# Three of eight feature tiles of a depthwise convolution as products with diagonal matrices

## The chip, the cores and the metric

One core of one Trainium2 chip. The time is that of one execution of the whole program on the device, in microseconds (us); of several runs the median is told.

## What is computed

A network of two blocks on 256 tokens of 1024 features, batch 1. The second block has two layers, and in layer 0 two streams go through the same mixer: the context (`ctx`) first, whose keys, values and states the latent stream's mixer then uses. In layer 1 only the latent stream has a mixer. Each mixer has three branches (attention, gated linear attention, convolution), which are gated, summed and projected:

```python
def _conv_module(glu, p):
    a, g = jnp.split(glu, 2, axis=-1)
    y = a * jax.nn.sigmoid(g)
    pad = CONV_WIDTH // 2                      # CONV_WIDTH = 31
    y = lax.conv_general_dilated(y, p['conv_w_dw'], (1,), [(pad, pad)],
                                 dimension_numbers=('NWC', 'WIO', 'NWC'),
                                 feature_group_count=CONV_CH) + p['conv_b_dw']
    y = jax.nn.silu(_layernorm(y, p['conv_ln_g'], p['conv_ln_b']))
    return y @ p['w_conv_o']
```

The convolution is depthwise: each of 1024 features has its own 31 taps over the tokens, and the layer norm after it runs over all features. So it needs all eight tiles of features.

## The kernel before, in words

Everything is kept with features on the 128 partitions and 256 tokens along them, so 1024 features are eight tiles (`KT`). A weight comes in units of 128x1024 f32 (`unit`, L438): SyncE loads `raw`, ScalarE rounds it to `whi`, VectorE or GpSimd subtracts to `wlo` (`load`, L455; in the mixer three of five subtractions go to GpSimd by `lo_eng`, L373). An ordinary product (`mm3`) is three runs of eight matmuls in the reduced format: `whi` with the high part of the input (`hh`, `yh`), `whi` with its low part (`hl`, `yl`), `wlo` with the high part; 24 matmuls to a unit. Their sums lie in three PSUM banks, `mm`. All small products (attention, gated linear attention or GLA) are in full f32, and their results share four PSUM banks of the pool `at` (`ps`, L414).

The convolution (`conv`, L1372) takes a tile `yp` of 128x286 (256 tokens with 15 zeros at each side), which `glu` (L1384) makes, and adds 31 taps on VectorE: one `tensor_scalar` with the first weight and the bias, then 30 `scalar_tensor_tensor` that multiply the shifted tile by a weight per feature and add it to the sum `ca`. The taps have a priority lowered by 1000, so that the scheduler puts them where VectorE has nothing else.

`mix` (L1395) sets the order in which the branches are written: a loop of 16 rounds with steps of attention (`att`), of `side` (the projections for GLA, with `glu` between), of the first GLA pair (`gla[0]`, one step for each of its eight levels) and of the convolution; then the first gated branch with the second GLA pair and the convolution; then the projections `r`, whose products with the GLA output make `yg`; then the second gated branch, the end of the convolution and its layer norm (`ln_core`, L603), and the third gated branch. This is not the order on the engines. A scheduler takes what is written, gives out the buffers of a pool in the order in which they are asked for, and lists the instructions of each engine by priority and its own estimate; each engine then runs its list in order.

Names in the rows: `mm` a projection's sum; `lg`, `pt`, `av` attention's logits, transposed weights and output; `gz`, `gt`, `gs`, `ga`, `ov` GLA's gates, transposition, state, scores of a level and output; `gF` a level's factors; `st` sums for norms; `hsq` squares; `fsum`, `sq` the layer norm's; `acc` the sum of the branches.

Of the kernel before, what the change touches and what calls it, by code (L numbers as in the profile page):

```python
# [10 lines left out]
F32 = mybir.dt.float32  # L11
# [3 lines left out]
AF = mybir.ActivationFunctionType  # L15
# [3 lines left out]
P = 128  # L19
D = 1024  # L20
T = 256
# [251 lines left out]
def run(*gens):  # L273
    for g in gens:
        for _ in g:
            pass


def step(g, n):
    for _ in range(n):  # L280
        if next(g, g) is g:
            return False
    return True
# [38 lines left out]
class Builder:  # L322
# [1046 lines left out]
                                       lambda ov, f=f + i: self.psplit(ov[:, :T], y[0][:, f], y[1][:, f]))  # L1369
                yield  # L1370

    def conv(self, l, yps, ca):  # L1372
        for ft, yp in enumerate(yps):
            o = ca[:, ft]
            w = lambda i: self.pvc(f"dw{l}", i * 8 + ft)
            self.ts(o, yp[:, 0:T], w(0), self.pvc(f"dwb{l}", ft), ALU.mult, ALU.add)
            for i in range(1, 31):
                with self.tc.high_priority(offset=-1000):
                    self.stt(o, yp[:, i:i + T], w(i), o, ALU.mult, ALU.add)
                if i % 8 == 7:  # L1380
                    yield
            yield

    def glu(self, l, h, yps):  # L1384
# [10 lines left out]
    def mix(self, l, h, x, ada, mem, bp, keep, then=None):  # L1395

        nc = self.nc  # L1400
        self.act(x, x, scale=ALPHA)
        qk, vg, glr, gates, pairs = self.gla_in(l, h, bp, True)
        S = mem[2] if mem else None
        new_S = None if mem else keep.tile([P, 2, 4, T], F32, tag="S", name="S")
        gla = [self.gla_pair(l, hp, qk, vg, glr, S, new_S) for hp in range(2)]
        run(gates)
        kt, vt = self.kv_in(l, h, bp if mem else keep, "x" if mem else "")
        if mem:
            self.rope(kt)
        yps = [bp.tile([P, T + 30], F32, tag="yp", name="yp", bufs=8) for _ in range(KT)]  # L1410
        newy = lambda: self.new_y(bp)
        ya = newy()
        ca = self.hp.tile([P, KT, T], F32, tag="D", name="ca")
        acc = None

        def gated(n, y):
            return self.gated_all(f"gb{n}_{l}", h, y, acc, n == 0, [0.0] * KT)
        att = self.attention(l, h, ya, kt, vt, mem, bp)
        conv = self.conv(l, yps, ca)
        side = chain(pairs[0], self.glu(l, h, yps), pairs[1])  # L1420
        step(att, 1)
        for i in range(16):
            step(att, 1)
            step(side, 1)
            step(att, 1)
            if i >= 2:
                step(gla[0], 1)
            if i >= 4:
                step(conv, 1)
        run(att, side, gla[0])  # L1430

        acc = bp.tile([P, 4, T], F32, tag="vg", name="acc", bufs=2)
        acc = [acc[:, f] for f in range(4)]
        for _ in range(2):
            a = bp.tile([P, 2, T], F32, tag="q", name="acc", bufs=2)
            acc += [a[:, 0], a[:, 1]]
        acc = Tiles(acc)
        g0 = gated(0, ya)
        for _ in range(8):
            step(gla[1], 2)  # L1440
            step(g0, 1)
            step(conv, 2)
        run(gla[1], g0)
        self.some_f32 = False
        yg = newy()
        for f in range(0, KT, 2):
            ps = self.pair(f"r{l}", f, h)
            s = self.t("sr", 512)
            self.act(s, ps, AF.Silu)
            for j in range(2):  # L1450
                sj = s[:, j * T:(j + 1) * T]
                if self.native:
                    self.tt(yg[0][:, f + j], sj, qk[:, f // 2, j], ALU.mult, nc.gpsimd)
                else:
                    self.tt(sj, sj, qk[:, f // 2, j], ALU.mult, nc.gpsimd)
                    self.split(sj, yg[0][:, f + j], yg[1][:, f + j])
            step(conv, 2)
        g1 = gated(1, yg)
        step(g1, 3)
        run(conv)  # L1460
        yc = newy()
        r = self.ln_core(ca, ca)
        for f in range(KT):
            t = self.t("ht")
            self.stt(t, ca[:, f], self.pvc(f"clg{l}", f), r, ALU.mult, ALU.mult)
            self.act(yc[0][:, f] if self.native else t, t, AF.Silu, bias=self.pvc(f"clb{l}", f))
            if not self.native:
                self.split(t, yc[0][:, f], yc[1][:, f])
            if f in (0,2,4,6):
                step(g1, 1)  # L1470
        g2 = gated(2, yc)
        run(g1)
        step(g2, 8)
        if then:
            step(then, 1)
        run(g2)
        mx = newy()
        self.halve(acc, mx)
        for f in range(0, KT, 2):
            if then:  # L1480
                step(then, 2)
            ps = self.pair(f"out{l}", f, mx)
            for j in range(2):
                self.stt(x[:, f + j], ps[:, j * T:(j + 1) * T], ada[:, 16 + f + j:17 + f + j], x[:, f + j],
                         ALU.mult, ALU.add)
        if then:
            run(then)
        run(self.post(x, f"l1g{l}", f"l1b{l}", l == 1))
        return kt, vt, new_S
# [148 lines left out]
```

## Time and profile before

| | us |
|---|---|
| median of 3 runs | 3063.51 |
| lowest and highest of them | 3053.55, 3064.5 |
| the profiled execution | 3057.49 |
| its span | 3055.3 |
| TensorE busy | 2805.1 |
| VectorE busy | 2004.4 |
| ScalarE busy | 1408.2 |
| GpSimd busy | 923.8 |

The span is what the profile shows of one execution, from its first instruction to its last; about 2 us lie around it. Busy times are of that execution alone, which is not one of the three runs. A busy engine isn't always the one that is waited for: what counts is which engine lets the others wait in the stage that is changed.

### The profile page before, as it was taken

The page shows a single profiled execution, that of the slowest core. Times are in us where ns is not written, and L with a number is a line of the kernel's source. Part 1 is how long each engine was busy: PE and PEld are TensorE (multiplying, and loading weights), DVE is VectorE, ACT ScalarE, POOL GpSimd, SP SyncE. Part 2 cuts the span into 40 slices and gives each one's busy share as a digit, 9 for nine tenths or more (in the row PEclk, how much of TensorE's full clock was granted, in tenths as well). Part 3 has the DMA queues.
Part 4 walks back from the last instruction along what each step waited for, and adds up shares of the span by engine and source line. Part 5 has one row for each costly group of instructions (what it writes and reads, how often), then busy time and mean ns, then how long its engine had stood idle before and what let it go on. Part 6 is the DMA issues. An engine that isn't in the chain of part 4 may idle for free.

```text
span 3055.3 us, 51829 instructions
## 1 busy us (share of the span) xinstructions
PE 2805.1 (92%) x20816; PEld 2626.8 (86%) x20816; DVE 2004.4 (66%) x3305; ACT 1408.2 (46%) x2127; POOL 923.8 (30%) x684
## 2 busy tenths in 40 slices
PE   7998889999998878799999999999999999998898
PEld 6897778888898778788899988998898788898898
DVE  7597763347855999956798344467344499674554
ACT  5464456544445434345645554445434332354443
POOL 3243322233324444641102104444320113453000
PEclk9999999999999989899999999999999999999999
DMA  5443334566456554688567986654643223344353
GB/s 196 146 159 130 125 112 177 179 250 246 154 203 237 193 211 173 238 304 287 210 233 249 330 307 254 239 188 172 250 147 119 97 97 124 118 161 144 126 180 109
DMA packets 153425, 578.32 MB, mean 189 GB/s; under 512 B 17628, under 2 KB 17756, under 8 KB 146656
## 3 DMA queue, kind: packets, MB, share of 16 engines
q1 hardware_dynamic: 152496, 574.45, 53.2%
q8 instruction: 163, 2.67, 0.3%
q14 instruction: 78, 0.64, 0.1%
q10 hardware_dynamic: 688, 0.56, 0.1%
HBM read 516.73 MB, written 58.20 MB: 188 GB/s over the span
## 4 chain that ended last, share of the span: by engine, by line
PE 46%; DVE 19%; ACT 4%; DMA 2%; issue 1%; POOL 1%; SPq 0%; DVEq 0%; ACTq 0%; POOLq 0%
PE mm L371 38%; DVE ca L364 7%; PE st L371 2%; DVE gF L361 2%; DMA raw<-in_ws 2%; PE av L371 1%; DVE sq L361 1%; PE ga L371 1%; DVE wlo L361 1%; PE ad L371 1%; POOL wlo L361 1%; DVE fsum L572 1%; ACT whi L358 1%; PE ov L371 1%; PE lg L371 1%
## 5 line engine op out<-in xcount | busy, mean ns | idle before, releaser
L358 ACT ACTIVATE whi<-raw 128x1024 fp32r<-128x1024 f32 (+1 forms) x706 | 735.9, 1045 | 838.5 <-PE mm L371 529.3
L361 POOL TENSOR_TENSOR wlo<-raw,whi 128x1024 fp32r<-128x1024 f32 (+1 forms) x282 | 717.1, 2545 | 1046.1 <-ACT whi L358 825.6
L361 DVE TENSOR_TENSOR wlo<-raw,whi 128x1024 fp32r<-128x1024 f32 (+1 forms) x315 | 397.7, 1263 | 356.9 <-ACT whi L358 345.8
L371 PE MATMUL mm<-hh,whi 128*128 128x256 f32 x3376 | 504.6, 291 | 18.9 <-ACT hh L358 5.5
L371 PE MATMUL mm<-hh,wlo 128*128 128x256 f32 x3376 | 495.7, 288 | 15.2 <-DVE wlo L361 10.1
L371 PE MATMUL mm<-hl,whi 128*128 128x256 f32 x3376 | 493.0, 288 | 0.0
L371 PEld LDWEIGHTS mm<-hh,whi 128*128 128x128 f32 x3376 | 448.9, 196 | 43.7 <-issue 9.0
L371 PEld LDWEIGHTS mm<-hh,wlo 128*128 128x128 f32 x3376 | 448.4, 196 | 18.5 <-DVE wlo L361 10.5
L371 PEld LDWEIGHTS mm<-hl,whi 128*128 128x128 f32 x3376 | 446.9, 195 | 3.8 <-issue 3.1
L364 DVE SCALAR_TENSOR_TENSOR ca<-yp,pv,ca 128x256 f32<-128x256 f32 x720 | 360.9, 556 | 2.0
L371 PE MATMUL mm<-yh,whi 128*128 128x256 f32 x1152 | 174.6, 291 | 14.6 <-ACT yh L358 10.1
L371 PE MATMUL mm<-h,raw 128*128 128x256 f32 x800 | 181.9, 381 | 0.0
L361 POOL TENSOR_TENSOR gF<-cum 128x128 f32<-128x128 f32 x192 | 99.8, 550 | 255.0 <-PE ga L371 142.0
L371 PEld LDWEIGHTS mm<-yh,whi 128*128 128x128 f32 x1152 | 154.6, 195 | 21.2 <-ACT yh L358 13.2
L371 PE MATMUL mm<-yh,wlo 128*128 128x256 f32 x1152 | 168.1, 288 | 4.9 <-DVE wlo L361 3.9
L371 PE MATMUL mm<-yl,whi 128*128 128x256 f32 x1152 | 168.7, 288 | 2.6 <-DVE yl L364 2.6
L371 PEld LDWEIGHTS mm<-h,raw 128*128 128x128 f32 x800 | 150.3, 191 | 19.3
L371 PEld LDWEIGHTS mm<-yh,wlo 128*128 128x128 f32 x1152 | 152.4, 196 | 6.8 <-DVE wlo L361 4.1
L371 PEld LDWEIGHTS mm<-yl,whi 128*128 128x128 f32 x1152 | 152.9, 195 | 3.3 <-DVE yl L364 2.8
L371 PE MATMUL mm<-hidh,whi 128*128 128x256 f32 x704 | 102.9, 287 | 0.5 <-ACT hidh L358 0.5
L371 PE MATMUL mm<-hidl,whi 128*128 128x256 f32 x704 | 102.2, 286 | 0.0
L371 PE MATMUL mm<-hidh,wlo 128*128 128x256 f32 x704 | 101.5, 285 | 0.0
(280 smaller groups left out, 3840.6 us busy)
## 6 DMA issues: line engine op xcount, KB each, us to landing
raw<-in_ws SPq DMA_DIRECT2D x744, 512.0 KB, 3.8
lo<-wlo SPq DMA_DIRECT2D x109, 512.0 KB, 3.0
wlo<-lo SPq DMA_DIRECT2D x109, 512.0 KB, 4.2
wada<-in_wa SPq DMA_DIRECT2D x48, 1024.0 KB, 5.9
raw<-in_ws SPq DMA_DIRECT2D x32, 384.0 KB, 3.0
memt<-in_tok SPq DMA_DIRECT2D x4, 256.0 KB, 4.7
xt<-in_tok SPq DMA_DIRECT2D x1, 1024.0 KB, 7.1
ct<-in_tok SPq DMA_DIRECT2D x1, 1024.0 KB
```

The source lines that it names most:

```text
L358: return self.nc.scalar.activation(out, in_, f, **k)
L361: return (eng or self.nc.vector).tensor_tensor(out=out, in0=a, in1=b, op=op)
L364: return self.nc.vector.scalar_tensor_tensor(out=out, in0=a, scalar=s, in1=b, op0=op0, op1=op1)
L371: return self.nc.tensor.matmul(out, lhsT=l, rhs=r, start=start, stop=stop, **k)
L572: self.nc.vector.tensor_reduce(out=s, in_=x.rearrange("p f n -> p n f"), axis=AX.X, op=ALU.add)
```

## The change

In layer 0's ctx mixer (the one whose `mem` is empty) `conv` leaves out tiles 2, 5 and 7, and `conv_pe` works them out. For each tap ScalarE writes a diagonal matrix (the identity, scaled by the tap's weight of each feature) into `dg`, which has two buffers of four matrices, and TensorE multiplies it by the shifted `yp` in full f32, 31 products summed in one half of a bank `cv` of the pool `at`. ScalarE adds the bias and writes the sum to `ca`. The products and the diagonals have the lowered priority of the taps. Two tiles share a bank, so there are two banks one after the other. The other two mixers are unchanged.

```diff
--- before.py
+++ after.py
@@ -1369,16 +1369,42 @@
                                        lambda ov, f=f + i: self.psplit(ov[:, :T], y[0][:, f], y[1][:, f]))
                 yield
 
-    def conv(self, l, yps, ca):
+    def conv(self, l, yps, ca, on_pe=()):
+
+        pe, n = self.conv_pe(l, yps, ca, on_pe), 0
         for ft, yp in enumerate(yps):
+            if ft in on_pe:
+                continue
             o = ca[:, ft]
             w = lambda i: self.pvc(f"dw{l}", i * 8 + ft)
             self.ts(o, yp[:, 0:T], w(0), self.pvc(f"dwb{l}", ft), ALU.mult, ALU.add)
             for i in range(1, 31):
                 with self.tc.high_priority(offset=-1000):
                     self.stt(o, yp[:, i:i + T], w(i), o, ALU.mult, ALU.add)
-                if i % 8 == 7:
+                if i % 8 == 7 or i == 30:
+
+                    n += 1
+                    if n > 3:
+                        step(pe, 1)
                     yield
+        run(pe)
+
+    def conv_pe(self, l, yps, ca, fts):
+
+        for k, ft in enumerate(fts):
+            if k % 2 == 0:
+                bank = self.ps("cv")
+            o = bank[:, k % 2 * T:k % 2 * T + T]
+            for i in range(0, 31, 4):
+                n = min(4, 31 - i)
+                dg = self.tmp[0].tile([P, 4, P], F32, tag="dg", name="dg", bufs=2)
+                with self.tc.high_priority(offset=-1000):
+                    for j in range(n):
+                        self.act(dg[:, j], self.cst("ident"), scale=self.pvc(f"dw{l}", (i + j) * 8 + ft))
+                        self.mm(o, dg[:, j], yps[ft][:, i + j:i + j + T], start=i + j == 0, stop=i + j == 30)
+                if i + n < 31:
+                    yield
+            self.act(ca[:, ft], o, AF.Identity, bias=self.pvc(f"dwb{l}", ft))
             yield
 
     def glu(self, l, h, yps):
@@ -1416,7 +1442,7 @@
         def gated(n, y):
             return self.gated_all(f"gb{n}_{l}", h, y, acc, n == 0, [0.0] * KT)
         att = self.attention(l, h, ya, kt, vt, mem, bp)
-        conv = self.conv(l, yps, ca)
+        conv = self.conv(l, yps, ca, () if mem else (2, 5, 7))
         side = chain(pairs[0], self.glu(l, h, yps), pairs[1])
         step(att, 1)
         for i in range(16):
```

How the order moves. Up to row 1250 TensorE's order is the same in both; from there TensorE's list before goes between the projections (`mm`) and the first GLA pair and attention (`lg`, `pt`, `av`, `ga`):

```order
L371 MATMUL lg<-kt,q 128x256 x2
L371 MATMUL ga<-gF 128x128 x4
L371 MATMUL mm<-hh,whi 128x256 x8
L371 MATMUL mm<-hl,whi 128x256 x8
L371 MATMUL mm<-hh,wlo 128x256
L656 MATMUL pt<-cc,pr 128x128
L371 MATMUL mm<-hh,wlo 128x256 x7
L371 MATMUL mm<-hh,whi 128x256 x8
L371 MATMUL mm<-hl,whi 128x256 x5
L656 MATMUL pt<-cc,pr 128x128 x3
L371 MATMUL mm<-hl,whi 128x256 x3
L371 MATMUL mm<-hh,wlo 128x256 x3
```

In the changed program projections alone follow there, 468 products in rows 1251 to 1320, and the end of that stretch reads so:

```order
L371 MATMUL mm<-yh,whi 128x256 x12
L371 MATMUL mm<-hh,whi 128x256 x8
L371 MATMUL mm<-hl,whi 128x256 x8
L371 MATMUL mm<-hh,wlo 128x256 x8
L371 MATMUL cv<-yp,dg 128x256
L656 MATMUL pt<-cc,pr 128x128 x4
L371 MATMUL mm<-yh,whi 128x256 x6
L371 MATMUL av<-ptsb,vt 128x256 x2
L371 MATMUL lg<-kt,q 128x256 x2
L371 MATMUL mm<-yh,whi 128x256 x3
L371 MATMUL cv<-yp,dg 128x256 x2
L371 MATMUL ga<-gF 128x128 x4
```

The attention head that stood at once behind row 1253 now stands behind the first convolution product, and with it the rest of the first GLA pair.

Further on TensorE's list before has the last levels of the second GLA pair, its output and norm between products of the first gated branch:

```order
L371 MATMUL mm<-hh,wlo 128x256 x8
L371 MATMUL mm<-yh,whi 128x256 x8
L371 MATMUL ga<-gF 128x128 x4
L371 MATMUL ga<-q_11995,qk 128x128 x4
L371 MATMUL mm<-yl,whi 128x256 x8
L371 MATMUL mm<-yh,wlo 128x256 x4
L371 MATMUL ov<-am,vg 128x256 x6
L371 MATMUL st<-hsq,ones 128x256 x2
L371 MATMUL ov<-am,vg 128x256 x2
L371 MATMUL mm<-yh,wlo 128x256 x4
```

and the changed one has them behind the projections `r` and 42 convolution products:

```order
L371 MATMUL mm<-hh,wlo 128x256 x8
L371 MATMUL cv<-yp,dg 128x256 x42
L371 MATMUL ga<-gF 128x128 x8
L371 MATMUL ga<-q_12094,qk 128x128 x4
L371 MATMUL cv<-yp,dg 128x256 x2
L371 MATMUL ov<-am,vg 128x256 x6
L371 MATMUL st<-hsq,ones 128x256 x2
L371 MATMUL ov<-am,vg 128x256 x2
L371 MATMUL cv<-yp,dg 128x256 x2
L371 MATMUL st<-hsq,ones 128x256 x2
L371 MATMUL cv<-yp,dg 128x256 x8
L371 MATMUL mm<-hh,whi 128x256 x8
```

They moved from within the first gated branch to behind most of `r`.

On VectorE, where before the taps stand in short runs between weight subtractions (`wlo`), levels (`am`, `gF`) and attention:

```order
L364 SCALAR_TENSOR_TENSOR ca<-yp,pv,ca 128x256 x5
L361 TENSOR_TENSOR wlo<-raw,whi 128x1024
L364 SCALAR_TENSOR_TENSOR ca<-yp,pv,ca 128x256 x5
L364 SCALAR_TENSOR_TENSOR yp<-gt,mm 128x256
L364 SCALAR_TENSOR_TENSOR ca<-yp,pv,ca 128x256
L1233 COPY_PREDICATED am<-gm,ga 128x2x2x128
L368 TENSOR_SCALAR ca<-yp,pv 128x256
L364 SCALAR_TENSOR_TENSOR ca<-yp,pv,ca 128x256 x5
L361 TENSOR_TENSOR wlo<-raw,whi 128x1024
L364 SCALAR_TENSOR_TENSOR ca<-yp,pv,ca 128x256 x6
```

the changed list has, while TensorE does the projections above:

```order
L361 TENSOR_TENSOR wlo<-raw,whi 128x1024
L364 SCALAR_TENSOR_TENSOR ca<-yp,pv,ca 128x256 x13
L361 TENSOR_TENSOR wlo<-raw,whi 128x1024
L364 SCALAR_TENSOR_TENSOR ca<-yp,pv,ca 128x256 x18
L361 TENSOR_TENSOR wlo<-raw,whi 128x1024
L364 SCALAR_TENSOR_TENSOR ca<-yp,pv,ca 128x256 x18
L361 TENSOR_TENSOR wlo<-raw,whi 128x1024
L361 TENSOR_TENSOR yl<-av,yh 128x256
L641 TENSOR_REDUCE nm<-lg 128x1
L364 SCALAR_TENSOR_TENSOR ca<-yp,pv,ca 128x256
```

The taps of the five tiles stand in long runs ahead of the attention's `yl` and `nm`, and the last of them right behind.

## Rows read from the trace of the kernel before

**Rows 1.** The page, part 1: busy time, share of the span, instructions.

```profile
PE 2805.1 (92%) x20816; PEld 2626.8 (86%) x20816; DVE 2004.4 (66%) x3305; ACT 1408.2 (46%) x2127; POOL 923.8 (30%) x684
```

**Rows 2.** The page, part 4: the chain of waits, share of the span by line.

```profile
PE mm L371 38%; DVE ca L364 7%; PE st L371 2%; DVE gF L361 2%; DMA raw<-in_ws 2%; PE av L371 1%; DVE sq L361 1%; PE ga L371 1%; DVE wlo L361 1%; PE ad L371 1%; POOL wlo L361 1%; DVE fsum L572 1%; ACT whi L358 1%; PE ov L371 1%; PE lg L371 1%
```

**Rows 3.** Windows: stretch, its us, busy us by engine, granted clock, DMA share, GB/s.

```profile
1036.90:1314.10 277.20, 219.45 (x1588) 211.81 (x1586) 261.37 (x411) 108.46 (x153) 142.29 (x112) 0.90 0.59 208
...
1036.90:1116.10 79.20, 67.23 (x480) 64.20 (x478) 78.70 (x148) 29.73 (x44) 31.41 (x28) 0.91 0.55 196
...
1198.00:1274.00 76.00, 60.02 (x456) 58.56 (x455) 72.25 (x99) 25.96 (x36) 48.20 (x32) 0.91 0.59 205
```

**Rows 4.** Tile `ca`, 989 to 1296 us: ns min/median/max, first start, last.

```profile
L364 DVE SCALAR_TENSOR_TENSOR ca<-yp,pv,ca x240: 459/474/2670, 989.1 to 1267.1; 128x256 f32<-128x256 f32 x120
...
L572 DVE TENSOR_REDUCE fsum<-ca x1: 3615/3615/3615, 1274.1 to 1274.1; 128x256 f32<-128x2048 f32 x1
...
L364 DVE SCALAR_TENSOR_TENSOR ca<-st,ca x1: 2278/2278/2278, 1279.9 to 1279.9; 128x2048 f32<-128x2048 f32 x1
```

**Rows 5.** Timeline of VectorE: start us, us, instruction, count.

```profile
1001.76 2.57 DVE L364 SCALAR_TENSOR_TENSOR ca<-yp,pv,ca 128x256 f32<-128x256 f32 x1
...
1049.51 1.26 DVE L364 SCALAR_TENSOR_TENSOR ca<-yp,pv,ca 128x256 f32<-128x256 f32 x3
...
1094.77 5.61 DVE L364 SCALAR_TENSOR_TENSOR ca<-yp,pv,ca 128x256 f32<-128x256 f32 x14
```

**Rows 6.** Timeline of GpSimd, around the first row above.

```profile
1001.44 2.60 POOL L361 TENSOR_TENSOR wlo<-raw,whi 128x1024 fp32r<-128x1024 f32 x1 [3.13 <-ACT whi L358]
```

**Rows 7.** Lines, 1036 to 1296 us: count, busy us, mean ns, idle before.

```profile
L364 DVE SCALAR_TENSOR_TENSOR ca<-yp,pv,ca 128x256 f32<-128x256 f32 x207 | 129.2, 679 | 0.2
...
L361 POOL TENSOR_TENSOR wlo<-raw,whi 128x1024 fp32r<-128x1024 f32 x33 | 98.5, 2988 | 63.0 <-ACT whi L358 33.8 <-ACT hsq L358 15.2 <-ACT gF L358 4.8
...
L361 DVE TENSOR_TENSOR wlo<-raw,whi 128x1024 fp32r<-128x1024 f32 x18 | 22.1, 1226 | 2.0 <-ACT whi L358 1.3 <-issue 0.6
...
L361 DVE TENSOR_TENSOR gF<-gF,qk 128x1024 f32<-128x1024 f32 x11 | 17.9, 1631 | 0.2 <-ACT gF L358 0.2
```

**Rows 8.** Timeline of TensorE: start us, us, instruction, count, idle before.

```profile
1037.96 1.12 PE L371 MATMUL mm<-hl,whi 128*128 128x256 f32 x8
...
1038.92 0.28 PE L371 MATMUL mm<-hh,wlo 128*128 128x256 f32 x1
...
1051.10 1.03 PE L371 MATMUL lg<-kt,q 128*128 128x256 f32 x4
...
1061.23 1.13 PE L371 MATMUL av<-ptsb,vt 128*128 128x256 f32 x4
...
1114.55 1.89 PE L371 MATMUL gz<-glr,w 128*128 128x256 f32 x8
...
1144.14 0.69 PE L1289 MATMUL gt<-cc,gw 128*128 128x128 f32 x2 [8.50 <-DVE gw L361]
...
1148.38 1.89 PE L371 MATMUL gs<-vg,gkt 128*128 128x256 f32 x8
...
1150.11 0.60 PE L1289 MATMUL gt<-cc,gw 128*128 128x128 f32 x4
...
1289.56 0.67 PE L371 MATMUL st<-sq,ones 128*128 128x256 f32 x2 [2.16 <-DVE sq L361]
...
1314.09 1.22 PE L371 MATMUL mm<-hh,whi 128*128 128x256 f32 x8 [2.17 <-DVE gt L364]
```

**Rows 9.** Lines by form, whole span: ScalarE's 128x128 activations.

```profile
L358 ACT ACTIVATE fs<-fs,fnm 128x128 f32<-128x128 f32 x16 | 6.3, 396 | 3.1 <-DVE fnm L939 3.1
...
L358 ACT ACTIVATE sw<-z 128x128 f32<-128x128 f32 x16 | 4.2, 261 | 0.0
```

**Rows 10.** Windows, tile `ca` alone, between two rows of TensorE above.

```profile
1114.55:1144.14 29.59, 13.30 (x22) 0.00 (x0) 0.83 0.58 206
```

## The prediction

> **What bounds the kernel now.** The page comes first: TensorE is busy for 92% of the span and VectorE for 66% [rows 1], so over the whole program TensorE is the bound. The chain of waits, read next, gives the place where that isn't so: the matmuls hold most of it, but second among its lines are the convolution's taps, `DVE ca`, with 7% [rows 2]. There are three mixers with a convolution, and only the first, the ctx mixer of layer 0, is changed. The busy time by stage is then read for it: from 1036.9 to 1314.1 us VectorE is busy 261.4 of 277.2 us and TensorE 219.5; in the first 79 us of that, VectorE has half a microsecond free [rows 3]. So here VectorE sets the pace and TensorE waits some 58 us (277.2 less 219.5). Of the convolution's own instructions the tile view shows 240 taps in this mixer, each 0.47 us in the median, and one of 2.67 [rows 4].
>
> I take that window because 1036.9 us is where TensorE's order first differs between the two programs, and 1314.1 us is the start of the first row from which on both have done the same products (row 1490 before, 1505 now).
>
> **What the change removes.** Three of eight feature tiles leave VectorE: 90 taps and 3 first taps. Fourteen taps in a row take 5.61 us [rows 5], 0.395 us each when they follow each other, so 93 x 0.395 = 37 us of VectorE. A tap that meets a GpSimd subtraction is longer: the one at 1001.76 takes 2.57 us and ends 0.3 us after the subtraction begun at 1001.44 [rows 5, 6]. The mean tap of this stretch is 0.679 us [rows 7], which over 207 taps is 42 us above the median tap, or 1.3 us for each of the 33 GpSimd subtractions; a single meeting costs 2.57 - 0.47 = 2.1.
>
> **What it adds.** 93 matmuls of 128x256 in full f32. Eight matmul records of that kind start 1.73 us before the next row, 0.216 each, and one product is two records [rows 8]: 0.43 us, so 40 us of TensorE. The ordinary product of this kernel (eight from 1037.96 to 1038.92 [rows 8]) is 0.12 us. So TensorE gets a little more than VectorE loses. ScalarE makes 93 diagonal matrices of 128x128; the two nearest rows are 0.261 and 0.396 us [rows 9]. I take 0.3, because an ordinary copy lies between: 28 us in all, 24 to 37 by the bounds, and below TensorE's 0.43 in each case. ScalarE has room, and on the way to the end it only counts where TensorE has nothing but these products. Three evictions on ScalarE (128x256) are some 1 us.
>
> **What it moves** decides. In the new order TensorE runs all that remains of the projections (`glu`, k, q and v of the second pair, the first gates), 468 products, before the first convolution product, and two attention heads, four levels of the first GLA pair and its output stand behind that; before, they stood in between. The convolution's bank comes from the same four PSUM banks (`at`), is asked for ahead of theirs, and its products have the lowest priority. In the same way the last two levels of the second GLA pair stand behind 42 convolution products in one row. VectorE on the other side does 107 of the 150 taps of its five tiles at a stretch. So the sum is made by stages, in TensorE's new order.
>
> 1. To the first convolution product's neighbours. TensorE needs 468 x 0.12 = 56 us. VectorE gets to its run of taps at about 1049.5, where before the attention's and level's work ends too [rows 5]. From there it has 107 taps (42.3), 8 weight subtractions at 1.14 without overlap (9.1; the row's 1.23 [rows 7] contains some) and 2 us of others: 53.3 us. GpSimd makes 11 subtractions meanwhile; at 1.7 us each, between the 1.3 and the 2.1 above, +19 (14 to 23). VectorE is done with it at 1122. TensorE waits for weights behind the runs of 20, 13 and 18 taps, arrives at about 1110 and then needs VectorE for the next attention maximum.
> The Trainium skill, "SBUF — State Buffer", section "Who interferes with whom", says that a VectorE instruction with two SBUF inputs and a GpSimd instruction that reads SBUF exclude each other, and that the later one waits for the whole of the other. By it alone each of the 11 would cost the full 2.1, and the sum would be 4 us higher; the rows agree on the exclusion, and the mean shows that not all of them meet a tap.
> 2. The postponed pieces, now one behind the other. From the logits to the product with the values took 10.1 us before (1051.10 to 1061.23 [rows 8]), some 3 of them taps; I take 8. Two levels of 4 us (the last multiplication alone is 1.63 in the mean, taps beside it [rows 7]; building and exponential come ahead of it), 1 us of copies, and 16 f32 products for output, norm and gates of the second pair (6.9): 24 us, to 1146.
> 3. The second GLA pair. From its gates' product to the first transposition took 29.6 us (1114.55 to 1144.14 [rows 8]), with 13 us of taps in between [rows 10]; without them 17. Of this stage's 58.8 us of products (384 ordinary ones 46.1, state and levels 9.7, seven of the convolution 3.0) 12.5 are done during the 17; the other 46, and 5 us of waits for six levels, follow: to 1214.
> 4. 54 convolution products 23.3, the last levels, output and norm 7.7, two waits of about 1 us: 33.5, to 1247.5. VectorE has next to nothing to do here.
> 5. 14 units of 2.88: 12 for the rest of r and the gates, 29 for y, then the last 19 convolution products 8.2: to 1296.
> 6. The layer norm over channels, which is now alone: in the new order no product stands between the last convolution product and the norm's two sums. Before it went from 1274.1 (the reduction) to 1289.6 (the second sum), 15.5 us [rows 4, 8], of which some 5 went to other work. I take 11, with 3.6 and 2.3 for the two long instructions [rows 4]: to 1307.
> 7. Five units 14.4: to 1321.5, against 1314.1 now: **7.5 us later**. The norm's result then comes 17 us before it is wanted where before it had 28: 3 us more of waiting (0 to 8).
>
> Sum: +40 us of products on TensorE, and 30 of its waits go: **+10.5 us** on 3057.5 us, the profiled execution's time. That execution is 6.0 us below the median of the three runs (3063.5), so on the median I write 3074. The forecast's own range is the bounds above: VectorE's meetings with GpSimd 4 us either way, stage 3's waits 0 to 12, stage 6 at 9 to 15, stage 2's levels at 3 to 5 us, and stage 1 up to 12 us shorter if GpSimd fits into gaps: 3053 to 3092. Nothing else is charged: the weight loads and their queue are the same transfers in the same order, and the first two groups of diagonals are made far ahead, on an idle ScalarE.
>
> **The rivals.** *The relief arrives* (faster). VectorE's 261 us fall by 37 and by a share of the meetings; TensorE needs 219.5 + 40 = 259.5, of which some 22 are time at the lower of its two clock levels (the granted clock is 0.90 of full here [rows 3]) behind waits. With full speed in most of the stretch and 20 us of waits instead of 58 it takes 237 + 20 = 257 instead of 277, and the time is 3043. For it speaks that VectorE really is the limit in every stage of rows 3. Against it speaks that the removed 37 us are needed evenly, while the new order gives VectorE its taps all in stage 1 and leaves it empty in stages 4 and 5.
>
> *The diagonal products set the pace* (slower). In stages 4 and 5, 73 of these products stand in rows with little else. There are two buffers of four diagonals; TensorE uses a group in 1.73 us. If a diagonal takes 0.396 us [rows 9] and the hand-over to and fro adds 1 us to each group, a group takes 2.6, and 15 groups cost 13 us more. The lower clock costs 22 us in this stretch now, in which TensorE's timeline has a dozen waits of over 2 us, so about 2 us each; six new ones are 12 more. With the forecast's +10.5 that is +35: 3099. It decides once ScalarE needs over 0.43 us a diagonal with its waits. For it: every such group crosses engines twice. Against it: ScalarE is less than half busy in all of these stages.
>
> *The edit doesn't take effect* is excluded by the order: 93 products fewer on VectorE and 93 on TensorE. That the mixer's end is hidden is excluded too: the next mixer starts with its result, and the chain of waits runs through it.
>
> **Chances.** The forecast 0.50, of which most lies within 15 us of the median, since it is +10.5 with bounds of -10 and +28; the relief 0.14; the diagonals 0.28; and 0.08 for other mixtures, near no change. A measurement of this kernel can tell about 0.5%, 15 us, from no change. That makes faster 0.13, same 0.47, slower 0.40. The range goes from the relief's time to the diagonals': 3040 to 3102.
>
> **What would show it.** Right: VectorE's taps in a dense block up to about 1122, TensorE waiting 15 us or so for weights in it; attention and levels behind 1110; 42 `cv` products in a row near 1215 with VectorE idle; a wait of about 10 us before the norm's sums, near 1300. Wrong: taps without meetings and a first convolution product before 1100 (then the relief), or `cv` products more than 0.5 us apart (then the diagonals).

## The result, and the profile after

Four runs of the changed kernel had a median of 3087.2 us (3084.55 to 3094.24) beside 3059.6 for the kernel before: a ratio of 1.0084, 95% interval 1.0067 to 1.0101. It is **0.84% slower**, some 26 us; the two profiled executions are 3084.55 and 3057.49 us. The forecast was +10.5 us. The page, part 1, beside [rows 1]:

```profile
PE 2839.2 (92%) x21002; PEld 2657.3 (86%) x21002; DVE 1949.2 (63%) x3212; ACT 1438.2 (47%) x2223; POOL 925.4 (30%) x684
```

VectorE lost 55 us, TensorE gained 34, and the span grew by 27. The windows of the changed mixer (stretch, its us, then busy us of PE, PEld, DVE, ACT, POOL, granted clock, DMA share, GB/s) answer to [rows 3]; the last row is the whole of it, from the row where the orders part to the first row after which both have done the same products:

```profile
1036.90:1116.10 79.20, 62.13 (x462) 61.05 (x461) 76.94 (x134) 24.03 (x31) 43.20 (x22) 0.87 0.62 219
1116.10:1153.20 37.10, 32.00 (x192) 28.05 (x191) 23.64 (x49) 16.72 (x35) 10.19 (x16) 0.95 0.49 179
1153.20:1225.70 72.50, 62.51 (x471) 60.84 (x470) 54.29 (x75) 37.73 (x49) 43.69 (x43) 0.93 0.61 220
1225.70:1258.50 32.80, 32.24 (x160) 27.59 (x159) 6.70 (x9) 20.40 (x57) 1.42 (x7) 1.00 0.19 65
1258.50:1312.20 53.70, 50.58 (x374) 48.73 (x373) 21.96 (x21) 25.32 (x46) 31.41 (x20) 0.97 0.74 268
1312.20:1348.10 35.90, 19.71 (x125) 17.96 (x124) 20.68 (x33) 13.47 (x26) 10.60 (x8) 0.71 0.27 90
1036.90:1348.10 311.20, 259.16 (x1773) 244.22 (x1771) 204.20 (x318) 137.66 (x241) 140.51 (x112) 0.91 0.54 192
```

The stretch takes 311.2 us instead of 277.2. TensorE is busy for 259.2 instead of 219.45, which is the forecast's 40 us; but it still waits 52.0 us where it waited 57.7. VectorE was to be freed and is: 204 of 311. TensorE hardly profits.

TensorE's timeline shows the places (start us, us, instruction, count, idle before):

```profile
1073.92 2.07 PE L371 MATMUL mm<-hh,wlo 128*128 128x256 f32 x8 [6.09 <-DVE wlo L361]
...
1117.63 0.60 PE L371 MATMUL cv<-yp,dg 128*128 128x256 f32 x2
...
1151.48 1.03 PE L371 MATMUL gz<-glr,w 128*128 128x256 f32 x4
...
1172.03 0.66 PE L1289 MATMUL gt<-cc,gw 128*128 128x128 f32 x2 [6.10 <-DVE gw L361]
...
1225.72 4.92 PE L371 MATMUL cv<-yp,dg 128*128 128x256 f32 x22
1231.20 13.65 PE L371 MATMUL cv<-yp,dg 128*128 128x256 f32 x62 [0.56 <-ACT ca L358]
...
1303.96 8.37 PE L371 MATMUL cv<-yp,dg 128*128 128x256 f32 x38
...
1316.52 1.22 PE L371 MATMUL st<-fsum,ones 128*128 128x256 f32 x2 [4.19 <-DVE fsum L572]
...
1324.35 1.19 PE L371 MATMUL st<-sq,ones 128*128 128x256 f32 x2 [6.61 <-DVE sq L361]
...
1329.99 2.08 PE L371 MATMUL mm<-hh,whi 128*128 128x256 f32 x8 [4.45 <-DVE gt L364]
...
1348.12 1.22 PE L371 MATMUL mm<-hh,whi 128*128 128x256 f32 x8 [0.96 <-DVE gt L364]
```

and VectorE's timeline the other side of it:

```profile
1079.21 12.30 DVE L364 SCALAR_TENSOR_TENSOR ca<-yp,pv,ca 128x256 f32<-128x256 f32 x20
...
1110.40 3.45 DVE L361 TENSOR_TENSOR wlo<-raw,whi 128x1024 fp32r<-128x1024 f32 x1 [2.26 <-ACT whi L358]
...
1125.68 0.42 DVE L361 TENSOR_TENSOR yl<-av,yh 128x256 fp32r<-128x256 f32 x1
...
1245.78 0.73 DVE L1233 COPY_PREDICATED am<-gm,ga 128x512 f32<-128x512 uint8 x1 [18.51 <-PE ga L371]
...
1312.87 3.59 DVE L572 TENSOR_REDUCE fsum<-ca 128x256 f32<-128x2048 f32 x1 [7.31 <-ACT ca L358]
```

All that the forecast named is there: the block of taps to 1125.7; waits for weights (`wlo`) in it; the convolution's row of 42 products (two records each, 22 and 62) with VectorE idle for 18.5 us; the norm's sums with nothing to cover them. After them, behind waits of 4.19, 6.61 and 4.45 us, the granted clock is 0.71 of full in the mean of the last stretch, between the two levels, and eight products take 2.08 us at 1329.99 against 1.22 at 1348.12.

The row at 1348.12 answers to the one of before at 1314.09 [rows 8]: 34.0 us later. Of these 5.5 come back in the next 90 us, where TensorE waits 6.1 us in all instead of 8.5 and has a granted clock of 1.00 in the first 52 us against 0.97; 27 are left at the end.

### The profile page after: what moved, and what is told of

Same layout as the page of the kernel before. It is cut to its first block, busy times and chain, and to the rows that moved or that the text cites. A ratio compares the mean times of both kernels' runs of the same rounds, so it can differ in the third digit from the quotient of the medians.

```text
span 3082.6 us, 52227 instructions
## 1 busy us (share of the span) xinstructions
PE 2839.2 (92%) x21002; PEld 2657.3 (86%) x21002; DVE 1949.2 (63%) x3212; ACT 1438.2 (47%) x2223; POOL 925.4 (30%) x684
## 5 line engine op out<-in xcount | busy, mean ns | idle before, releaser
L364 DVE SCALAR_TENSOR_TENSOR ca<-yp,pv,ca 128x256 f32<-128x256 f32 x630 | 300.7, 539 | 2.2
```

The lines of the kernel that those rows point to most:

```text
L364: return self.nc.vector.scalar_tensor_tensor(out=out, in0=a, scalar=s, in1=b, op0=op0, op1=op1)
```

## The experiments

Each kernel is compared with the kernel before on the same chip. Told is the ratio of the times with its 95% interval in brackets, and the ratio as microseconds of 3062, about the median of the kernel before.

**The first four kernels.** The first theory was *order*: the 40 us of products are paid for by VectorE's relief, and what costs is where the scheduler put things. Its rivals were *products* (40 us on TensorE cost what they cost anywhere) and *diagonals* (the hand-over from ScalarE).

`normal_priority`, in `conv_pe`:

```diff
-                with self.tc.high_priority(offset=-1000):
+                if True:
```

> The change with one edit: the convolution's products and diagonals are written at normal priority instead of the lowered one; VectorE's taps keep theirs. In TensorE's list attention and the levels then stand where they stood before the change, with four convolution products between one level and the next, and all 93 are done ahead of the second GLA pair's output. Theory 'order' (what costs is that attention, levels and norm were put behind projections and products, not the 40 us of products themselves): faster than before by 15 us (0 to 25). Rival 'products' (40 us more on TensorE cost what they cost wherever they stand): still 20 to 30 us slower than before. Rival 'diagonals' (the hand-over from ScalarE sets the pace): still 15 to 27 us slower, since the same 93 diagonals are made.

Measured: 1.0026 (1.0015 to 1.0038), +8.0 us. No theory had that: undoing the order is worth some 18 us, but leaves a kernel that is still slower.

`quarter_products`:

```diff
-                    for j in range(n):
+                    for j in range(1):
...
-                        self.mm(o, dg[:, j], yps[ft][:, i + j:i + j + T], start=i + j == 0, stop=i + j == 30)
+                        self.mm(o, dg[:, j], yps[ft][:, i + j:i + j + T], start=i == 0, stop=i == 28)
```

> The change with one product and one diagonal of every four: 24 instead of 93. Left out are the other 69 taps of tiles 2, 5 and 7. TensorE's order is the one of the change (bank asked for ahead, lowered priority, 468 projections first, two levels behind the second gated branch's r), only that the norm's sums stand 123 projections further back, as in the kernel before. 'order': 69 products less, at 0.43, are 30 us less on TensorE, but only those that stand in rows (some 54 of them, 23 us) and the exposed norm (12 us) come off the time: 5 to 10 us faster than before, and 20 us or more slower than the kernel without any of the products. 'products': the change's +27 less 30, 3 us faster than before, and 10 us slower than the kernel without products.

Measured: 0.9966 (0.9952 to 0.998), 10.4 us faster.

`constant_matrix`:

```diff
-                dg = self.tmp[0].tile([P, 4, P], F32, tag="dg", name="dg", bufs=2)
+                pass
...
-                        self.act(dg[:, j], self.cst("ident"), scale=self.pvc(f"dw{l}", (i + j) * 8 + ft))
-                        self.mm(o, dg[:, j], yps[ft][:, i + j:i + j + T], start=i + j == 0, stop=i + j == 30)
+                        self.mm(o, self.cst("ident"), yps[ft][:, i + j:i + j + T], start=i + j == 0, stop=i + j == 30)
```

> The change with the constant identity in place of the diagonals: no diagonal is made on ScalarE, the 93 products stay and the order of TensorE too. Left out are the tap weights of tiles 2, 5 and 7. 'order' and 'products': within 5 us of the change, 22 to 30 us slower than before. 'diagonals': 10 to 20 us faster than the change.

Measured: 1.0089 (1.0073 to 1.0106), the same as the change. *Diagonals* is out. The tile view says it too, of the change's diagonals and of this kernel's products (ns min/median/max):

```profile
L358 ACT ACTIVATE dg<-cc,pv x93: 384/387/402, 863.8 to 1309.9; 128x128 f32<-128x128 f32 x93
```

```profile
L371 PE MATMUL cv<-yp,cc x186: 377/378/631, 1120.3 to 1313.9; 128*128 128x256 f32 x186
```

`no_products`, in `conv_pe`:

```diff
-            for i in range(0, 31, 4):
...
-            self.act(ca[:, ft], o, AF.Identity, bias=self.pvc(f"dwb{l}", ft))
+            for i in range(0, 28, 4):
+                yield
+            self.act(ca[:, ft], yps[ft][:, 15:15 + T], AF.Identity, bias=self.pvc(f"dwb{l}", ft))
```

> The change without bank, diagonals and products: ScalarE fills the three tiles from the middle of yp. Left out is the convolution of tiles 2, 5 and 7. TensorE's order is that of before to within a few projections. It bounds the relief on VectorE. 'order': VectorE's 37 us and a share of the meetings come off a stretch that VectorE bounds, 35 us faster than before (25 to 45). 'products': the change's +27 less 40 us of products, 13 us faster than before (8 to 18).

Measured: 0.9935 (0.9921 to 0.995), **19.9 us faster**, neither 35 nor 13. With 37 us of taps gone, the meetings that went with them, and nothing in their place, 20 us is all that is won. And `quarter_products`, in the change's order with 10 us of products, is only 9.5 us behind it: *order* as first stated falls too, since an order that costs 20 should show there.

Why only 20? The view of TensorE's waits (waiting line, released by: us in total, times, longest), for the changed stretch of the kernel before:

```profile
PE mm L371 <- DVE wlo L361: 14.0, 3, 9.3
PE ga L371 <- DVE gF L361: 9.3, 3, 4.8
PE gt L1289 <- DVE gw L361: 8.5, 1, 8.5
PE mm L371 <- POOL wlo L361: 5.9, 3, 4.8
PE ov L371 <- DVE am L1239: 5.6, 1, 5.6
PE pt L656 <- DVE nm L361: 4.3, 1, 4.3
```

and of `no_products`:

```profile
PE ga L371 <- DVE gF L361: 7.9, 4, 3.0
PE mm L371 <- DVE wlo L361: 6.4, 1, 6.4
PE ov L371 <- DVE am L1239: 6.2, 1, 6.2
PE gt L1289 <- DVE gw L361: 6.2, 2, 4.7
PE st L371 <- DVE sq L361: 5.3, 1, 5.3
PE pt L656 <- DVE nm L361: 4.4, 1, 4.4
```

Waits for **weights** (`wlo`), which stand behind the taps on VectorE, were 19.9 us and are 6.4. The waits for levels, gates, attention's maximum and output (27.7 us in these rows) are as long as before to within 3 us in all. I read them as chains across engines, each step waiting for the last, beside which VectorE's taps only filled the time; that is argued. So the second theory, *few waits*: only the waits for weights can be won, and everything that TensorE gets is paid from those 20 us.

**The next four.** `own_bank` separates the two parts of the order:

```diff
-        self.atp = ep(name="atp", bufs=4, space=bass.MemoryType.PSUM)
+        self.atp = ep(name="atp", bufs=3, space=bass.MemoryType.PSUM)
+        self.cvp = ep(name="cvp", bufs=1, space=bass.MemoryType.PSUM)
...
-                bank = self.ps("cv")
+                bank = self.cvp.tile([P, 512], F32, tag="cvb", name="cv")
```

> The change with a PSUM bank of its own for the convolution's products, taken from the pool of attention and levels, which keeps three; products and diagonals keep the lowered priority. Attention and all levels then stand in TensorE's list where they stood before the change, but 42 products stand in one row right ahead of the norm's two sums, with no product between these. So this has the exposed norm of the change without its postponed attention and levels. 'order' splits its 20 us (the change less the kernel at normal priority) into the norm, some 12, and the postponed work, some 8: 20 us slower than before (14 to 25). Rival 'all of it is the bank' (attention and levels asked for behind the convolution's bank are the whole 20): 8 us slower than before, like the kernel at normal priority. Rival 'lowered priority in itself': no less than the change's 27.

`before_three_banks` is its control, with only the 4 of the first line made 3, in the kernel before:

> The kernel before with three instead of four PSUM banks for attention and levels, nothing else: what the bank that the kernel above takes away costs. All theories: within 4 us of before. If it is more, the kernel above is read against this one.

Measured: 1.0073 (1.0058 to 1.0088), +22.4 us, and 1.0 (0.999 to 1.001) for the control. With attention and the levels back in place nearly all of the loss stays, so the bank and its queue are the smaller part. (The interval overlaps the change's own, 1.0067 to 1.0101.) The norm remains as the candidate.

`one_tile`: `normal_priority` with `(2,)` for `(2, 5, 7)`.

> One tile (2) instead of three on TensorE, at normal priority: 31 products, four after each level of the first pair. The kernel without products was 20 us faster, which is the 20 us that TensorE waited for weights behind the taps; its other 34 us of waits stayed. Theory 'few waits' (only the waits for weights behind the taps can be won, and the first tile taken off wins most of them): 12 us of relief less 13.3 us of products, of which a third comes back with the clock: 3 us faster than before (0 to 7). Rival 'relief in proportion' (each tile gives 6.5 us and costs 9): 3 us slower.

Measured: 0.9978 (0.9966 to 0.9989), **6.7 us faster**, at the upper end of what *few waits* had. The waits for weights in this stretch are now

```profile
PE mm L371 <- DVE wlo L361: 7.2, 3, 3.0
```

7.2 us instead of 19.9: of the waits for weights the first tile wins most.

`one_tile_placed`: the same, but the groups of products are taken out of `conv` and written where TensorE waited:

```diff
+        self.fill = self.conv_pe(l, yps, ca, on_pe)
...
+        if not hp:
+            step(self.fill, 3)
         st = self.st()
...
+            if hp and li in (0, 1, 2, 4, 5):
+                step(self.fill, 1)
             ps = self.ps("ga").rearrange("p (h b n) -> p h b n", h=2, n=P)
```

> One tile (2) at normal priority, its 31 products written where TensorE waited before for something other than weights: 12 right ahead of the first pair's output (5.6 us of wait), 8 at the second pair's transpositions (8.5 us), 11 between its levels (9.3 us). 'few waits': the relief of the kernel above, and the first 12 products, 5 us, lie in a wait: 8 us faster than before (3 to 12). 'relief in proportion': 1 us faster. If the place of the products is of no account: the same as the kernel above.

Measured: 0.999 (0.9981 to 1.0), 3 us faster: a miss, since 8 were expected. The wait that the products were to fill grew from 8.5 to

```profile
PE gt L1295 <- DVE gw L361: 12.1, 1, 12.1
```

since the scheduler now lists 78 projections between the gates and the transposition where it had 113. From gates to transposition takes 26.8 us here and 29.6 before [rows 8].

**The last four.** `norm_covered`, in `conv_pe`:

```diff
-                with self.tc.high_priority(offset=-1000):
+                with self.tc.high_priority(offset=-500):
```

> The change with one number: the products' and diagonals' priority is lowered by 500 instead of 1000. Attention and the first pair's levels still stand behind projections (524 of them instead of 660), the last two levels of the second pair still behind r, but the last products end some 90 projections ahead of the norm's two sums, which stand where they stood before. Theory 'norm' (most of what order costs is that no product stands between the convolution's end and the norm's sums): 11 us better than the change, 14 us slower than before (8 to 18). Rival 'postponed' (attention and levels behind projections are most of it): 22 to 27 us slower than before.

Measured: 1.0045 (1.003 to 1.0059), **+13.8 us**, as *norm* had it. Attention and levels are still postponed, and 12 of the 26 us are gone. TensorE's timeline shows the last product well ahead of the sums, and short waits at them, and the view of its waits has another change:

```profile
1274.94 7.07 PE L371 MATMUL cv<-yp,dg 128*128 128x256 f32 x32
...
1293.00 0.59 PE L371 MATMUL st<-fsum,ones 128*128 128x256 f32 x2
...
1303.18 1.05 PE L371 MATMUL st<-sq,ones 128*128 128x256 f32 x2 [2.16 <-DVE sq L361]
...
1329.10 1.22 PE L371 MATMUL mm<-hh,whi 128*128 128x256 f32 x8 [2.00 <-DVE gt L364]
```

```profile
PE mm L371 <- DVE wlo L361: 8.4, 2, 6.1
```

The waits at the norm (for `fsum`, `sq` and the `gt` behind them) are 4.2 us here and 16.2 in the change, which is the 12 us. But the waits for weights are also shorter, 8.4 us where the change has 17.1, and those for levels and `yl` longer (12.5 against 7.9): the edit moved all the products, so the norm's share is not shown alone.

`two_tiles`: `normal_priority` with `(2, 5)`.

> Two tiles (2 and 5) at normal priority, 62 products. 'few waits' (only the some 20 us of waits for weights can be won, and the first tile takes most of them): the second tile costs 9 us (13.3 less a third) and wins 3 to 4: 1 us faster to 3 slower than before. 'relief in proportion' (each tile moves the time by as much as the first, which gave 7): 14 us faster.

Measured: 0.9988 (0.9979 to 0.9997), 3.7 us faster, somewhat better than *few waits* had it. The first tile gave 6.7, the second takes some 3 back (the two intervals overlap), the third 11.7 more. *Relief in proportion* is out.

`one_tile_both_mixers`: `normal_priority` with `(2,) if l == 0 else ()`. The lines of the kernel before from 1487 to 1674 us, which hold the latent mixer's convolution (busy us, mean ns | idle before), have all 240 taps and not one weight subtraction:

```profile
L364 DVE SCALAR_TENSOR_TENSOR ca<-yp,pv,ca 128x256 f32<-128x256 f32 x240 | 103.3, 483 | 0.8
```

> One tile (2) at normal priority in both mixers of layer 0, the ctx and the latent one. In the latent mixer of the kernel before VectorE does the same 240 taps, at 0.483 us in the mean, and TensorE has no wait for weights at all from 1360 to 1800 us. 'few waits': nothing can be won there, so the 31 products cost their 13 us or a little less: 5 us slower than before (2 to 8), which is 12 slower than with one tile in the ctx mixer alone. 'relief in proportion' to the taps taken off VectorE: 13 us faster than before.

Measured: 1.0013 (1.0004 to 1.0023), +4.0 us, 10.7 behind `one_tile`. The same edit on the same taps wins 6.7 us in the ctx mixer and loses 10.7 in the latent one, where TensorE waits for no subtraction. (It does wait 8.2 us for rounded weights, `whi`, from ScalarE between 1360 and 1800 us, so the expectation's "no wait for weights at all" is too strong.) What this run can't tell is which waits made the difference: in the latent mixer TensorE hardly waits for anything, being busy for 181.2 of the 187 us from 1487 to 1674, where in the ctx mixer it is 219.5 of 277.2.

`one_tile_lowered`: the change with `(2,)` for `(2, 5, 7)`.

> The change with one tile (2) instead of three, at its lowered priority: attention and the first levels stand behind 660 projections as in the change; the last product ends 92 projections ahead of the norm's sums. 'norm': the order costs little where the norm is covered: 2 us faster than before (5 faster to 3 slower), 5 us behind the same tile at normal priority. 'postponed': 12 us behind it or more, so at least 5 us slower than before.

Measured: 0.9978 (0.9967 to 0.9989), 6.7 us faster, level with `one_tile`, where 2 us and 5 behind it were expected. And *few waits* as stated doesn't explain it: in this kernel TensorE waits 25.0 us for weights, more than the 19.9 of before,

```profile
PE mm L371 <- DVE wlo L361: 18.8, 4, 8.1
PE mm L371 <- POOL wlo L361: 6.2, 1, 6.2
```

while the waits for gates, attention's maximum and weights, and output (`gw`, `nm`, `pr`, `am`), 20.4 us before, are 1.5. In `quarter_products` too the waits for weights are 18.4 us, hardly shorter, and it is 10.4 us faster. So products can be paid for by other waits than those for weights, if the order puts them there. By the traces the postponement does cost inside the mixer: the row that ends it (1314.09 in [rows 8]) stands at 1313.63 here and at 1307.79 in `one_tile`, 5.8 us apart. Some 6 us are then made up in the 130 us behind the mixer; why stays open.

So, in microseconds of the whole time against before: three tiles off VectorE −19.9; their 93 products at normal priority +27.9, to +8.0; postponed and lowered, the norm still covered, +5.8, to +13.8; the norm uncovered (and what else the priority moves) some +12, to +25.7. At the row that ends the mixer, by the traces, the same four steps are −19.9, +24.8, +10.1 and +19.0, to +34.0; part of that comes back behind it. The version that beats both is one tile (`one_tile` or `one_tile_lowered`), by 0.2% of the kernel before.

## Why the prediction was right, and where its sizes were not

The direction and the range held, and every sign that the prediction named is in the trace; the size was +10.5 and came out as +26. **The step that failed is the sum's "+40 us of products on TensorE, and 30 of its waits go".** The 40 came (219.45 to 259.16). Of the waits 5.7 went (57.7 to 52.0). The view of TensorE's waits in the changed stretch has these among others:

```profile
PE mm L371 <- DVE wlo L361: 11.0, 3, 6.1
PE st L371 <- DVE sq L361: 6.6, 1, 6.6
PE mm L371 <- POOL wlo L361: 6.1, 1, 6.1
PE mm L371 <- DVE gt L364: 5.4, 2, 4.5
PE st L371 <- DVE fsum L572: 4.2, 1, 4.2
```

Sorted: the waits of the chains (levels, gates, attention) fell from 29.7 us to 14.0; those for weights only from 19.9 to 17.1, while VectorE's taps stand in one dense block (`own_bank`, which has attention and levels back in their places, has 5.4); those at the norm grew from 8.2 to 16.2; and 4.7 us of small ones are new. That many waits can go in another order: `normal_priority` loses 26.5 of them (31.2 left), with the products between a chain's steps. It still ends at +8.

Behind that stands the first paragraph's reading that VectorE "sets the pace" in this stretch. It was busy for 261 of 277 us, but with 37 us of taps and their meetings gone and nothing in their place, `no_products` still waits 41.5 us in its stretch and wins 19.9. That is less than the 93 products cost in any place tried (27.9 us at normal priority, the cheapest).

That the range held owes something to its width. The 3087.2 lie 13 us above the forecast's 3074 and 12 below the 3099 of a rival whose cause didn't hold; "same" had been given 0.47 and "slower" 0.40. Slips in the sums weigh little: stage 4's terms give 33.0 and not 33.5, stage 5's 49.2 and not 48.5, and 73 products are 18 groups of four, not 15, which makes the diagonals' price 16 us instead of 13 and their time 3102.

By stages, against the forecast's times at the same rows:

- *Stages 1 and 2*, to 1153.2 instead of 1146: +7. VectorE's block ended at 1125.7 (1122 forecast). Less taps, subtractions, others and a wait of 2.26 for a rounded weight, which the forecast had not, the meetings with GpSimd cost 20.6 us; 19 were forecast for 11, and ten were met. That is 2.1 each, the full price of the single meeting. So in this dense block the rule of the Trainium skill, "SBUF — State Buffer", section "Who interferes with whom" (the later one waits for the whole of the other), was the better guide than the mean of the rows. That a subtraction can also wait behind taps that begin after it, as one seems to do in the last section, isn't in it. TensorE's weight waits were 17.1 (15 forecast). The postponed pieces took 27.5 us, not 24.
- *Stage 3*, 72.5 instead of 68 us: gates to first transposition took 20.6 us from the second of the two gates' products (1151.48 to 1172.03), 22.4 from the first, without taps, where 17 was worked out by taking the 13.3 us of taps [rows 10] off the 29.6, which count from the first. So the taps were not all on the way.
- *Stage 4*, 32.8 instead of 33.5: a product at 0.43 us was right (62 records in 13.65).
- *Stage 5*, 53.7 instead of 48.5: 14 units took 45.5, not 41, of which 3.1 are waits for inputs and weights.
- *Stages 6 and 7*, 35.9 instead of 28.5, the largest: the norm alone took 12.5 (11 forecast), the wait on its result 5.4 (3 forecast), and the five units ran in part at the lower clock, 0.71 over the stretch, which no term held.

Together 23.6 us over the +10.5, so 34.0 at the row; 7 were regained behind it, which the forecast didn't have either.

The rivals. *The relief arrives* gave 3043 with all products on TensorE; the kernel without any of them is at 3044. It was out of reach. *The diagonal products set the pace* was nearer in time (+35) for a reason that didn't hold: 0.387 us a diagonal, below the 0.43 of a product, and no gain without them. Of its second part, a lower clock behind new waits, some showed, in stage 7.

## What to carry to other kernels

Before work is moved off a busy engine, measure what its absence is worth, with a kernel that leaves it out: here 20 us for 37 us of taps, on an engine that was busy for 94% of the stretch. Then split the waits of the engine that takes the work by what they wait for. Without anything in place of the taps it was mostly the waits for weights behind them that went (13.5 of 16.2 us); the waits of other chains went only in kernels that have products, and only in some orders. Move as much as that pays for and no more: here one tile of 13 us paid, and three of 40 didn't. Where the other engine had hardly a wait, the same edit was a loss. And work with the lowest priority, put on another engine, ends last there: look what waits for the last piece, and what would have covered that.

## What the runs showed of the hardware

A GpSimd subtraction can wait through many taps before it gets its turn. The shortest of the changed stretch takes 2.36 us, one of the usual length 2.49, the longest 7.05:

```profile
1064.55 2.49 POOL L361 TENSOR_TENSOR wlo<-raw,whi 128x1024 fp32r<-128x1024 f32 x1 [0.84 <-DMA lo<-wlo]
...
1094.07 7.05 POOL L361 TENSOR_TENSOR wlo<-raw,whi 128x1024 fp32r<-128x1024 f32 x1
```

On VectorE beside it

```profile
1092.57 5.22 DVE L364 SCALAR_TENSOR_TENSOR ca<-yp,pv,ca 128x256 f32<-128x256 f32 x13
...
1098.84 9.29 DVE L364 SCALAR_TENSOR_TENSOR ca<-yp,pv,ca 128x256 f32<-128x256 f32 x18
```

the first 13 taps run at 0.40 us each, undisturbed, to 1097.79; the next 18 take 2.2 us more than 18 x 0.395. So, by these lengths, the subtraction stood still for some 4.5 us, and then VectorE for 2.2. TensorE paid for it: its wait of 6.11 us at 1101.18 is for this `wlo`. Here the dense block of taps didn't only lengthen itself, it held back the engine that shares the weights' work.

TensorE gets back part of what it is given. In `normal_priority` the stretch has 40 us more of products, and TensorE is busy for only 32 us more than in [rows 3], so a fifth comes back, where the expectations of `one_tile` and `two_tiles` reckoned with a third: the granted clock is 0.95 there against 0.90, with products in former waits (stretch, its us, busy us as above, clock):

```profile
1036.32:1319.04 282.72, 251.49 (x1772) 238.86 (x1771) 198.70 (x318) 135.85 (x241) 131.20 (x112) 0.95 0.58 204
```
